# Score maxima taken as scaled, negated minima in the mask instruction, and mean squares moved from VectorE to GpSimd

## The chip, the cores and the metric

The kernel runs on one core of one Trainium2 chip, as one program. The metric is the device time of one execution in microseconds. One execution in the middle of such runs was profiled: its trace gives every instruction of TensorE (PE, with its weight loads as PEld), VectorE (DVE), ScalarE (ACT), GpSimd (POOL) and SyncE (SP, which issues the DMAs) with its start and its duration.

## The reference

The reference is a two-layer decoder trunk on x of shape (1, 256, 1024) in float32. Layer A is causal differential attention with 8 heads, each with two score maps c = 0, 1 of head dimension 64; layer B is dilated sliding-window attention with 16 heads in three groups of keys. Each layer is followed by a squared-ReLU MLP of width 4096. What matters here:

```
rms_norm(y, g) = y * rsqrt(mean(y*y) + EPS) * g        # over each head's 64 columns for q and k
A: s = q k^T * 64^-0.5, masked with -inf above the diagonal;  p = softmax(s)
   a = p[c=0] - lam * p[c=1];  o = rms_norm(a v, sub_gain) * (1 - lam_init)   # over 128 columns
B: s = q k^T * 64^-0.5 for three key groups, masked; m = max(s); p = exp(s - m);
   outputs of the groups mixed by their softmax denominators (one softmax over all groups)
x = x + att @ w_o;   x = x + square(relu(rms_norm(x) @ w_up)) @ w_down
```

## The kernel before

All matrix products are done in split form: each float32 operand is a high part and a low part, and three products are summed (high x high, high x low, low x high). The weights are split while the kernel runs. `Weights.split_half` (L73) lets ScalarE copy the high part of half a weight chunk (`whi`, L82) and VectorE subtract it from the raw chunk (`wlo`, L83); 272 such pairs are spread over the whole kernel, ahead of the products that use them. SyncE fetches the raw chunks by DMA.

The order of the stages is layer A, its output projection, MLP 0, layer B, its output projection, MLP 1. In A the loop runs over 8 heads, in B over 8 pairs of heads. For each, TensorE computes the projections (`gemm`, L297, products on L292 to L294), `qk_rows` (L310) makes normalised and rotated rows of q and k, and a generator, `attn_A` or `attn_B`, is started that does the attention of that head in steps. A generator yields numbers (`WAIT_A`, `WAIT_B`): so many ticks later its next step is put into the program. A tick comes after each half of a projection, so the attention of one head lies between the projection products of the next. The program is then planned by a scheduler that orders the instructions of each engine by their place in the program and by when it reckons that their operands are ready; each engine works through its own queue in that order, and waits at its head.

`qk_rows`, called twice per head in A and four times per pair in B (48 calls), works so: ScalarE squares (L315), VectorE multiplies the rows by the tables into `T` (L317) and sums the squares (`ss`, L321), VectorE forms the mean square plus a term, `ms` (L323), GpSimd adds the rotated halves (L328), raises `ms` to -0.5 (`f`, L332) and multiplies (`qn`, L334). Later TensorE transposes `qn` (L357), and ScalarE and VectorE split the transpose into `th` and `tl` (L340, L341), from which the scores are computed (`scores2`, L350).

The scores are masked by one VectorE instruction (`masked`, L369): it adds the mask to the scores in PSUM, writes the sum and takes its maximum over the row, `mx`. A tiny VectorE instruction then makes `nm`, minus the maximum times 64^-0.5 (L538 in A, L616 in B). ScalarE's exponential takes `nm` as its bias and 64^-0.5 as its scale, and sums the denominators (L541 in A, L618 in B). In B the reciprocal of the denominators (`rd`, L621) and the scaling of the probabilities (L623) follow, and then the transposes L632, the products with v (L646), and, for each pair of heads, a sum `oT` on GpSimd (L651), which ScalarE and VectorE split (L340, L341). In A the two maps are first combined (L545 to L549), transposed (L554) and multiplied by v (L565, L566); the output row is squared with a row sum (L574), its mean square `ms` formed on VectorE (L576), raised to -0.5 on GpSimd (`ors`, L578), applied on ScalarE (L580), and transposed (L584). `cf[:, :, 1]` (L547) is EPS times the square of the first map's denominator, which L576 adds.

The output projection's products are L402 to L404; the MLP's are L435, L437 and L488 to L490.

Of the kernel before, what the change touches and what calls it, by code (L numbers as in the profile page):

```python
# [10 lines left out]
F32 = mybir.dt.float32  # L11
F32R = mybir.dt.float32r
AF = mybir.ActivationFunctionType
ALU = mybir.AluOpType
AX = mybir.AxisListType

P = 128
S = 256
# [3 lines left out]
HD = 64  # L22
# [80 lines left out]
def trunk(ctx, tc, a):  # L103
# [206 lines left out]
    def qk_rows(ps, nsub, eps, tab):  # L310


        n = nsub * HD
        sq = wk.tile([P, 384], F32, name="sq", tag="sq")
        nc.scalar.activation(sq[:, :n], ps[:, :n], AF.Square)  # L315
        T = wk.tile([P, 2, 384], F32, name="T", tag="T")
        nc.vector.tensor_tensor(T[:, :, :n].rearrange("p c (h d) -> p c h d", h=2),  # L317
                                ps[:, None, :n].to_broadcast([P, 2, n]).rearrange("p c (h d) -> p c h d", h=2),
                                tab, op=ALU.mult)
        ss = small.tile([P, 8], F32, name="ss", tag="ss")  # L320
        nc.vector.reduce_sum(ss[:, :nsub], sq[:, :n].rearrange("p (h d) -> p h d", d=HD), axis=AX.X)  # L321
        ms = small.tile([P, 8], F32, name="ms", tag="ms")
        nc.vector.tensor_scalar(ms[:, :nsub], ss[:, :nsub], 1.0 / HD, eps, op0=ALU.mult, op1=ALU.add)  # L323
        u = T[:, 0]
        t1 = T[:, 1, :n]
        swapped = bass.AP(tensor=t1.tensor, offset=t1.offset + HD // 2,
                          ap=[t1.ap[0], [HD, nsub], [-(HD // 2), 2], [1, HD // 2]])
        nc.gpsimd.tensor_tensor(  # L328
            u[:, :n].rearrange("p (h a d) -> p h a d", a=2, d=HD // 2),
            T[:, 0, :n].rearrange("p (h a d) -> p h a d", a=2, d=HD // 2), swapped, op=ALU.add)  # L330
        f = small.tile([P, 8], F32, name="f", tag="f")
        nc.gpsimd.tensor_tensor(f[:, :nsub], ms[:, :nsub], half[:, :nsub], op=ALU.pow)  # L332
        qn = wk.tile([P, 384], F32, name="qn", tag="qn", bufs=6)
        nc.gpsimd.tensor_tensor(  # L334
            qn[:, :n].rearrange("p (h d) -> p h d", d=HD), u[:, :n].rearrange("p (h d) -> p h d", d=HD),
            f[:, :nsub, None].to_broadcast([P, nsub, HD]), op=ALU.mult)
        return qn
# [27 lines left out]

    KALL = slice(S, 2 * S)

    def masked(out, ps, m, init, mx):
        nc.vector.tensor_tensor_reduce(out, ps, m, 1.0, init, ALU.add, ALU.max, mx)  # L369


    def boundary(group, add, outs, ssx, first):
# [149 lines left out]
    def attn_A(hd, qr, kr, vt, oh, ol):  # L522
        yield WAIT_A[0]
        T = qk_T(qr, kr, (0, P))
        yield WAIT_A[1]
        mx = small.tile([P, 4], F32, name="mx", tag="mx")
        den = small.tile([P, 2, 2], F32, name="den", tag="den")
        sm = wk.tile([P, 2, 3 * P], F32, name="smA", tag="sm")
        scs = [wps(), wps()]
        scores2([sc[:, 0:S] for sc in scs], T, block(1), KALL)  # L530
        scores2([sc[:, S:S + P] for sc in scs], T, block(0), slice(S, S + P))
        for c in range(2):
            sc = scs[c]
            masked(sm[:, c, 0:S], sc[:, 0:S], mask[:, 8:10, :].rearrange("p b k -> p (b k)"),
                   -3e38, mx[:, 2 + c:3 + c])
            masked(sm[:, c, S:S + P], sc[:, S:S + P], mask[:, 9, :], -3e38, mx[:, c:c + 1])
        nm = small.tile([P, 4], F32, name="nm", tag="nm")
        nc.vector.tensor_scalar(nm, mx, -(HD ** -0.5), None, op0=ALU.mult)  # L538
        for c in range(2):
            for q, cols in ((1, slice(0, S)), (0, slice(S, S + P))):  # L540
                nc.scalar.activation(sm[:, c, cols], sm[:, c, cols], AF.Exp, bias=nm[:, 2 * q + c:2 * q + c + 1],  # L541
                                     scale=HD ** -0.5, accum_out=den[:, q, c:c + 1])

        cf = small.tile([P, 2, 2], F32, name="cf", tag="cf")
        nc.vector.reciprocal(cf[:, :, 0], den[:, :, 1])  # L545
        nc.vector.scalar_tensor_tensor(cf[:, :, 0], cf[:, :, 0], nlam, den[:, :, 0], op0=ALU.mult, op1=ALU.mult)
        nc.vector.scalar_tensor_tensor(cf[:, :, 1], den[:, :, 0], EPS, den[:, :, 0], op0=ALU.mult, op1=ALU.mult)  # L547
        for q, cols in ((1, slice(0, S)), (0, slice(S, S + P))):
            nc.vector.scalar_tensor_tensor(sm[:, 0, cols], sm[:, 1, cols], cf[:, q, 0:1], sm[:, 0, cols],  # L549
                                           op0=ALU.mult, op1=ALU.add)  # L550
        yield WAIT_A[2]
        pp = wps()
        for i in range(3):
            nc.tensor.transpose(pp[:, block(i)], sm[:, 0, block(i)], ident)  # L554
        p2 = wk.tile([P, 2, 3, P], F32R, name="pA", tag="p2")
        ph, pl = p2[:, 0], p2[:, 1]
        with tc.high_priority(100):
            split(ph, pl, pp[:, :384].rearrange("p (b q) -> p b q", b=3))
        yield WAIT_A[3]
        po = wps()  # L560
        for q in range(2):
            o2 = po[:, q * 2 * P:(q + 1) * 2 * P]
            for j in range(q + 1):
                b = j if q else 2
                nc.tensor.matmul(o2, ph[:, b], vt[:, j], start=j == 0, stop=False)  # L565
                nc.tensor.matmul(o2, pl[:, b], vt[:, j], start=False, stop=j == q)  # L566
        pov = po.rearrange("p (q l d) -> p q l d", q=2, l=2)
        oc = wk.tile([P, 2, P], F32, name="oc", tag="sq")
        nc.scalar.activation(oc, pov[:, :, 1, :], AF.Copy)
        orow = wk.tile([P, 2, P], F32, name="orow", tag="oT")  # L570
        nc.vector.tensor_tensor(orow, pov[:, :, 0, :], oc, op=ALU.add)
        oss = small.tile([P, 2], F32, name="oss", tag="oss")
        for q in range(2):
            nc.scalar.activation(oc[:, q, :], orow[:, q, :], AF.Square, accum_out=oss[:, q:q + 1])  # L574
        ms = small.tile([P, 8], F32, name="ms", tag="ms")
        nc.vector.scalar_tensor_tensor(ms[:, :2], oss, 1.0 / P, cf[:, :, 1], op0=ALU.mult, op1=ALU.add)  # L576
        ors = small.tile([P, 2], F32, name="ors", tag="ors")
        nc.gpsimd.tensor_tensor(ors, ms[:, :2], half[:, :2], op=ALU.pow)  # L578
        for q in range(2):
            nc.scalar.activation(orow[:, q, :], orow[:, q, :], AF.Copy, scale=ors[:, q:q + 1])  # L580
        yield WAIT_A[4]
        pt = wps()
        for q in range(2):
            nc.tensor.transpose(pt[:, block(q)], orow[:, q, :], ident)  # L584

        ptv = pt[:, :S].rearrange("p (m h l) -> p h m l", h=2, l=2)
        for t in range(NT):
            o = oh[:, hd, block(t)].rearrange("p (m l) -> p m l", l=2)
            nc.scalar.activation(o, ptv[:, t], AF.Copy, scale=sgain)
            nc.vector.scalar_tensor_tensor(ol[:, hd, block(t)].rearrange("p (m l) -> p m l", l=2), ptv[:, t], sgain,  # L590
                                           o.bitcast(F32), op0=ALU.mult, op1=ALU.subtract)
# [4 lines left out]
    def attn_B(hp, qr, kr, vts, oh, ol):  # L596
        yield WAIT_B[0]
        T0, T1, T2 = [qk_T(qr, kr, (c, c)) for c in (P, 0, 2 * P)]
        yield WAIT_B[1]
        mxs = [small.tile([P, 2], F32, name="mx", tag="mx") for _ in range(2)]  # L600
        sms = [wk.tile([P, 2, 4 * P], F32, name="sm", tag="sm") for _ in range(2)]
        for b in range(2):
            own = slice(S + b * P, S + (b + 1) * P)
            scs = [wps(), wps()]
            scores2([sc[:, 0:S] for sc in scs], T0, block(b), KALL)
            scores2([sc[:, S:S + P] for sc in scs], T1, block(b), own)
            scores2([sc[:, S + P:] for sc in scs], T2, block(b), own)
            for hh in range(2):
                masked(sms[hh][:, b, :], scs[hh], mask[:, 4 * b:4 * b + 4, :].rearrange("p b k -> p (b k)"),
                       -3e38, mxs[hh][:, b:b + 1])  # L610
            yield WAIT_B[2 + b]
        for hh in range(2):
            sm = sms[hh]
            den = small.tile([P, 2], F32, name="den", tag="den")
            nm = small.tile([P, 2], F32, name="nm", tag="nm")
            nc.vector.tensor_scalar(nm, mxs[hh], -(HD ** -0.5), None, op0=ALU.mult)  # L616
            for b in range(2):
                nc.scalar.activation(sm[:, b, :], sm[:, b, :], AF.Exp, bias=nm[:, b:b + 1], scale=HD ** -0.5,  # L618
                                     accum_out=den[:, b:b + 1])
            rd = small.tile([P, 2], F32, name="rd", tag="rd")  # L620
            nc.vector.reciprocal(rd, den)  # L621
# [209 lines left out]
```

## Time and profile before

| what | value |
|---|---|
| median of 3 runs | 800.8 us (800.39 to 802.36) |
| the profiled execution | 801.55 us, of which the span of instructions 799.5 us |
| TensorE busy | 772.1 us, 97% |
| VectorE busy | 581.1 us, 73%, 985 instructions |
| ScalarE busy | 467.0 us, 58% |
| GpSimd busy | 190.9 us, 24%, 191 instructions |
| mean share of the 16 DMA engines in q1 | 46.0% |

Times in the rows are microseconds from the start of the span, unless marked as ns. Busy time is a union, so that overlapping instructions count once; products on TensorE are pipelined and overlap by more than half. A wait is idle time of an engine ahead of an instruction, with the name of what released it behind "<-". The granted clock of TensorE (PEclk) is a share of full speed. Layer A with its output projection lies at about 10 to 135 us, MLP 0 up to 315, layer B with its projection up to 615, MLP 1 to the end.

### The profile page before, as it was taken

To read this page: it belongs to the slowest core of one execution; us is meant where nothing else is said; L and a number is where in the kernel's file an instruction comes from. 1 tells how busy PE (TensorE), PEld (TensorE's weight loads), DVE (VectorE), ACT (ScalarE), POOL (GpSimd) and SP (SyncE) were. 2 spreads that over 40 slices of the span, in tenths; PEclk is the share of its full clock that TensorE was granted. 3 is DMA by queue.
4 is the path that set the end of the run, shared out by engine and by line. 5 is a ranking of instruction groups with operands and counts; after the bars stand their busy time and mean duration, and the time that the engine had idled before them with its cause. 6 is when DMAs were issued, how large, how long until landed. Compare 5 with 4: busy or idle time off the path is not lost.

```text
span 799.5 us, 11766 instructions
## 1 busy us (share of the span) xinstructions
PE 772.1 (97%) x4408; PEld 686.7 (86%) x4408; DVE 581.1 (73%) x985; ACT 467.0 (58%) x851; POOL 190.9 (24%) x191
## 2 busy tenths in 40 slices
PE   6999989999999999999999999999997999999998
PEld 6898967888888888999999999999886888888886
DVE  3998987666656666998888888888767666556663
ACT  5667777544444445657586674857766544444441
POOL 2553531300000000555336354363611000000000
PEclk9999999999999999999999999999999999999999
DMA  8643445445555542554443434434442455545531
GB/s 300 229 143 123 158 155 164 169 171 197 198 176 207 171 184 90 187 198 154 136 153 113 157 121 157 158 119 172 159 158 106 158 186 182 210 170 199 187 130 52
DMA packets 22328, 131.12 MB, mean 164 GB/s; under 512 B 2560, under 2 KB 3328, under 8 KB 13056
## 3 DMA queue, kind: packets, MB, share of 16 engines
q1 hardware_dynamic: 22272, 130.38, 46.0%
q8 instruction: 34, 0.56, 0.3%
q14 instruction: 22, 0.18, 0.1%
HBM read 129.32 MB, written 1.05 MB: 163 GB/s over the span
## 4 chain that ended last, share of the span: by engine, by line
PE 64%; DVE 17%; ACT 12%; issue 3%; POOL 2%; DMA 1%; SPq 0%; POOLq 0%; DVEq 0%; ACTq 0%
PE wps L435 15%; PE wps L437 7%; PE acc L488 7%; PE acc L489 7%; PE acc L490 7%; DVE wlo L83 5%; PE acc L292 4%; PE acc L294 4%; PE acc L293 4%; ACT whi L82 4%; ACT sm L618 2%; DVE sm L369 2%; PE wps L632 2%; DVE T L317 2%; ACT smA L541 2%
## 5 line engine op out<-in xcount | busy, mean ns | idle before, releaser
L83 DVE TENSOR_TENSOR wlo<-raw,whi 128x1024 fp32r<-128x1024 f32 (+1 forms) x272 | 307.0, 1138 | 153.9 <-ACT whi L82 153.7
L82 ACT ACTIVATE whi<-raw 128x1024 fp32r<-128x1024 f32 (+1 forms) x272 | 258.9, 957 | 211.1 <-issue 74.9
L435 PE MATMUL wps<-hT,whi 128*128 128x512 f32 x512 | 182.2, 399 | 2.0 <-DVE hT L271 2.0
L437 PE MATMUL wps<-hT,wlo 128*128 128x256 f32 x512 | 142.9, 280 | 0.0
L435 PEld LDWEIGHTS wps<-hT,whi 128*128 128x128 f32 x512 | 95.9, 188 | 26.0 <-DVE hT L271 3.2
L328 POOL TENSOR_TENSOR T<-T 128x384 f32<-128x384 f32 (+1 forms) x48 | 44.4, 924 | 280.5 <-DVE ms L243 181.6
L488 PE MATMUL acc<-whi,u 128*128 128x512 f32 x256 | 100.4, 392 | 0.3 <-ACT u L340 0.3
L489 PE MATMUL acc<-wlo,u 128*128 128x512 f32 x256 | 100.0, 391 | 0.0
L490 PE MATMUL acc<-whi,u 128*128 128x512 f32 x256 | 98.9, 389 | 0.0
L437 PEld LDWEIGHTS wps<-hT,wlo 128*128 128x128 f32 x512 | 96.6, 189 | 1.4
L292 PE MATMUL acc<-whi,hT 128*128 128x384 f32 x256 | 88.8, 349 | 0.3 <-ACT whi L82 0.2
L292 PE MATMUL acc<-whi,hK 128*128 128x384 f32 x256 | 87.6, 343 | 0.0
L293 PE MATMUL acc<-wlo,hT 128*128 128x384 f32 x256 | 86.3, 337 | 1.1 <-DVE wlo L83 1.1
L294 PE MATMUL acc<-whi,hT 128*128 128x384 f32 x256 | 86.2, 337 | 0.0
L294 PE MATMUL acc<-whi,hK 128*128 128x384 f32 x256 | 85.8, 335 | 0.0
L293 PE MATMUL acc<-wlo,hK 128*128 128x384 f32 x256 | 85.7, 335 | 0.0
L332 POOL TENSOR_TENSOR f<-ms,half 128x6 f32<-128x6 f32 (+1 forms) x48 | 68.2, 1422 | 4.6 <-DVE ms L323 3.1
L488 PEld LDWEIGHTS acc<-whi,u 128*128 128x128 f32 x256 | 48.1, 188 | 11.7 <-ACT u L340 1.2
L490 PEld LDWEIGHTS acc<-whi,u 128*128 128x128 f32 x256 | 48.1, 188 | 10.6 <-DVE u L341 0.4
L489 PEld LDWEIGHTS acc<-wlo,u 128*128 128x128 f32 x256 | 48.1, 188 | 8.8
L293 PEld LDWEIGHTS acc<-wlo,hT 128*128 128x128 f32 x256 | 48.6, 190 | 1.4 <-DVE wlo L83 1.4
L292 PEld LDWEIGHTS acc<-whi,hT 128*128 128x128 f32 x256 | 48.6, 190 | 1.4 <-ACT whi L82 0.5
(117 smaller groups left out, 1204.9 us busy)
## 6 DMA issues: line engine op xcount, KB each, us to landing
raw<-in_wB SPq DMA_DIRECT2D x48, 768.0 KB, 4.2
raw<-in_wup SPq DMA_DIRECT2D x32, 1024.0 KB, 4.8
raw<-in_wdn SPq DMA_DIRECT2D x32, 1024.0 KB, 4.8
raw<-in_wA SPq DMA_DIRECT2D x15, 768.0 KB, 4.3
raw<-in_woA SPq DMA_DIRECT2D x4, 1024.0 KB, 4.8
raw<-in_woB SPq DMA_DIRECT2D x4, 1024.0 KB, 4.8
early<-in_x SPq DMA_DIRECT2D x2, 512.0 KB, 5.3
x<-in_xp SPq DMA_DIRECT2D x1, 1024.0 KB, 7.5
```

What stands on the lines that cost most here:

```text
L82: self.nc.scalar.activation(hi[:, :n], raw, AF.Copy)
L83: self.nc.vector.tensor_tensor(lo[:, :n], raw, hi[:, :n].bitcast(F32), op=ALU.subtract)
L292: nc.tensor.matmul(ps, h[:, kt, 0, tok], wh[:, c], start=kt == 0, stop=False)
L293: nc.tensor.matmul(ps, h[:, kt, 0, tok], wl[:, c], start=False, stop=False)
L294: nc.tensor.matmul(ps, h[:, kt, 1, tok], wh[:, c], start=False, stop=kt == KT - 1)
L328: nc.gpsimd.tensor_tensor(u[:, :n].rearrange("p (h a d) -> p h a d", a=2, d=HD // 2), T[:, 0, :n].rearrange("p (h a d) -> p h a d", a=2, d ...
L332: nc.gpsimd.tensor_tensor(f[:, :nsub], ms[:, :nsub], half[:, :nsub], op=ALU.pow)
L435: nc.tensor.matmul(o, wh[:, c], self.h[:, kt].rearrange("p l s -> p (l s)"), start=kt == 0, stop=False, skip_group_check=True)
L437: nc.tensor.matmul(o[:, 0:S], wl[:, c], self.h[:, kt, 0, :], start=False, stop=kt == KT - 1, skip_group_check=True)
L488: nc.tensor.matmul(ps, uh[:, tok], dh[:, c], start=first, stop=False)
L489: nc.tensor.matmul(ps, uh[:, tok], dl[:, c], start=False, stop=False)
L490: nc.tensor.matmul(ps, ul[:, tok], dh[:, c], start=False, stop=last)
```

## The change

The mask instruction now multiplies the masked sum by -(64^-0.5), writes that, and takes the minimum, which is at once `nm`; the separate `nm` instructions (8 in A, 16 in B) are gone and the exponential has scale -1. The mean square `ms` in `qk_rows` is computed by GpSimd. In A the term with the denominator is squared on ScalarE (scale EPS^0.5), the factor 1/128 of the output row's mean square moves into the scale of the ScalarE square, and the sum of both is taken on GpSimd.

```diff
@@ qk_rows
-        nc.vector.tensor_scalar(ms[:, :nsub], ss[:, :nsub], 1.0 / HD, eps, op0=ALU.mult, op1=ALU.add)
+        nc.gpsimd.tensor_scalar(ms[:, :nsub], ss[:, :nsub], 1.0 / HD, eps, op0=ALU.mult, op1=ALU.add)
@@ masked
-    def masked(out, ps, m, init, mx):
-        nc.vector.tensor_tensor_reduce(out, ps, m, 1.0, init, ALU.add, ALU.max, mx)
+    def masked(out, ps, m, nm):
+        nc.vector.tensor_tensor_reduce(out, ps, m, -(HD ** -0.5), 3e38, ALU.add, ALU.min, nm)
@@ attn_A
-        nm = small.tile([P, 4], F32, name="nm", tag="nm")
-        nc.vector.tensor_scalar(nm, mx, -(HD ** -0.5), None, op0=ALU.mult)
...
-                                     scale=HD ** -0.5, accum_out=den[:, q, c:c + 1])
+                                     scale=-1.0, accum_out=den[:, q, c:c + 1])
...
-        nc.vector.scalar_tensor_tensor(cf[:, :, 1], den[:, :, 0], EPS, den[:, :, 0], op0=ALU.mult, op1=ALU.mult)
+        nc.scalar.activation(cf[:, :, 1], den[:, :, 0], AF.Square, scale=EPS ** 0.5)
...
-            nc.scalar.activation(oc[:, q, :], orow[:, q, :], AF.Square, accum_out=oss[:, q:q + 1])
+            nc.scalar.activation(oc[:, q, :], orow[:, q, :], AF.Square, scale=P ** -0.5,
+                                 accum_out=oss[:, q:q + 1])
...
-        nc.vector.scalar_tensor_tensor(ms[:, :2], oss, 1.0 / P, cf[:, :, 1], op0=ALU.mult, op1=ALU.add)
+        nc.gpsimd.tensor_tensor(ms[:, :2], oss, cf[:, :, 1], op=ALU.add)
@@ attn_B
-            nm = small.tile([P, 2], F32, name="nm", tag="nm")
-            nc.vector.tensor_scalar(nm, mxs[hh], -(HD ** -0.5), None, op0=ALU.mult)
...
-                nc.scalar.activation(sm[:, b, :], sm[:, b, :], AF.Exp, bias=nm[:, b:b + 1], scale=HD ** -0.5,
+                nc.scalar.activation(sm[:, b, :], sm[:, b, :], AF.Exp, bias=nms[hh][:, b:b + 1], scale=-1.0,
```

## Rows read from the trace of the kernel before

**Rows 1.** The page's first part: busy time and share of each engine.
```profile
PE 772.1 (97%) x4408; PEld 686.7 (86%) x4408; DVE 581.1 (73%) x985; ACT 467.0 (58%) x851; POOL 190.9 (24%) x191
```
**Rows 2.** The list of waits: who waited for whom, total us, times, longest.
```profile
ACT smA L541 <- DVE nm L538: 14.6, 7, 2.8
...
PE wps L350 <- DVE tl L341: 4.1, 4, 1.9
...
PE wps L632 <- ACT sm L623: 3.9, 6, 1.0
...
PE acc L402 <- ACT oTh L340: 2.6, 1, 2.6
...
PE wps L357 <- POOL qn L334: 0.6, 1, 0.6
```
**Rows 3.** VectorE's timeline in one head of A: start, duration, instruction, [idle before].
```profile
83.42 0.41 DVE L369 CUSTOM_DVE_ANT_0 smA<-wps,mask 128x256 f32<-128x256 f32 x1
...
84.52 1.31 DVE L83 TENSOR_TENSOR wlo<-raw,whi 128x768 fp32r<-128x768 f32 x1
85.76 0.16 DVE L538 TENSOR_SCALAR nm<-mx 128x4 f32<-128x4 f32 x1
...
87.85 0.17 DVE L545 RECIPROCAL cf<-den 128x2 f32<-128x2 f32 x1 [0.72 <-ACT smA L541]
...
90.57 0.68 DVE L341 TENSOR_TENSOR tl<-wps,th 128x512 fp32r<-128x512 f32 x1
```
**Rows 4.** ScalarE's timeline in the same head.
```profile
85.95 0.51 ACT L541 ACTIVATE smA<-smA,nm 128x256 f32<-128x256 f32 x1 [2.68 <-DVE nm L538]
```
**Rows 5.** TensorE's timeline in the same head.
```profile
85.26 0.60 PE L357 MATMUL wps<-ident,qn 128*128 128x128 f32 x4
...
91.31 0.39 PE L350 MATMUL wps<-th,tl 64*128 64x256 f32 x2 [0.94 <-DVE tl L341]
```
**Rows 6.** GpSimd's timeline in the same head.
```profile
83.32 1.01 POOL L332 TENSOR_TENSOR f<-ms,half 128x4 f32<-128x4 f32 x1
84.41 0.61 POOL L334 TENSOR_TENSOR qn<-T,f 128x256 f32<-128x256 f32 x1
```
**Rows 7.** Timelines of four engines in one pair of heads of B.
```profile
392.16 0.73 POOL L651 TENSOR_TENSOR oT<-ot 64x256 f32<-64x256 f32 x1
...
398.76 0.28 DVE L616 TENSOR_SCALAR nm<-mx 128x2 f32<-128x2 f32 x2
...
398.96 0.72 ACT L618 ACTIVATE sm<-sm,nm 128x512 f32<-128x512 f32 x1 [1.83 <-DVE nm L616]
...
403.19 0.21 DVE L621 RECIPROCAL rd<-den 128x2 f32<-128x2 f32 x2
...
403.64 2.55 ACT L623 ACTIVATE sm<-sm,rd 128x512 f32<-128x512 f32 x4
...
404.40 1.27 PE L632 MATMUL wps<-ident,sm 128*128 128x128 f32 x8 [0.56 <-ACT sm L623]
```
**Rows 8.** Windows: stretch, length, busy of each engine, PEclk, DMA share, GB/s.
```profile
60.00:100.00 40.00, 37.16 (x250) 35.79 (x249) 36.68 (x105) 29.25 (x89) 17.71 (x23) 1.00 0.40 141
100.00:140.00 40.00, 35.85 (x184) 27.41 (x183) 32.38 (x82) 30.22 (x86) 8.41 (x11) 0.96 0.46 160
...
106.00:107.00 1.00, 1.00 (x2) 0.81 (x3) 1.00 (x5) 0.00 (x0) 0.90 (x2) 0.50 0.96 401
```
**Rows 9.** ScalarE's timeline in the last pair of heads of B.
```profile
594.89 0.72 ACT L618 ACTIVATE sm<-sm,nm 128x512 f32<-128x512 f32 x1 [2.94 <-DVE nm L616]
```
**Rows 10.** Instruction groups: busy us, mean ns of one, idle before and its releaser.
```profile
L323 DVE TENSOR_SCALAR ms<-ss,rB 128x6 f32<-128x6 f32 x32 | 9.9, 309 | 0.2
...
L576 DVE SCALAR_TENSOR_TENSOR ms<-oss,cf 128x2 f32<-128x2 f32 x8 | 1.2, 151 | 0.6 <-ACT oc L574 0.6
...
L203 ACT ACTIVATE le<-ls 128x2 f32<-128x2 f32 x1 | 0.2, 189 | 0.0
...
L172 POOL MEMSET half<- 128x8 f32 x1 | 0.1, 104 | 0.3 <-POOLq L821 0.3
```

More of the change, by code (lines that the diff above doesn't have):

```diff
@@ L525, in attn_A @@
         yield WAIT_A[1]
-        mx = small.tile([P, 4], F32, name="mx", tag="mx")
+        nm = small.tile([P, 4], F32, name="nm", tag="nm")
         den = small.tile([P, 2, 2], F32, name="den", tag="den")
@@ L534, in attn_A @@
             masked(sm[:, c, 0:S], sc[:, 0:S], mask[:, 8:10, :].rearrange("p b k -> p (b k)"),
-                   -3e38, mx[:, 2 + c:3 + c])
-            masked(sm[:, c, S:S + P], sc[:, S:S + P], mask[:, 9, :], -3e38, mx[:, c:c + 1])
-        nm = small.tile([P, 4], F32, name="nm", tag="nm")
-        nc.vector.tensor_scalar(nm, mx, -(HD ** -0.5), None, op0=ALU.mult)
+                   nm[:, 2 + c:3 + c])
+            masked(sm[:, c, S:S + P], sc[:, S:S + P], mask[:, 9, :], nm[:, c:c + 1])
         for c in range(2):
@@ L599, in attn_B @@
         yield WAIT_B[1]
-        mxs = [small.tile([P, 2], F32, name="mx", tag="mx") for _ in range(2)]
+        nms = [small.tile([P, 2], F32, name="nm", tag="nm") for _ in range(2)]
         sms = [wk.tile([P, 2, 4 * P], F32, name="sm", tag="sm") for _ in range(2)]
@@ L609, in attn_B @@
                 masked(sms[hh][:, b, :], scs[hh], mask[:, 4 * b:4 * b + 4, :].rearrange("p b k -> p (b k)"),
-                       -3e38, mxs[hh][:, b:b + 1])
+                       nms[hh][:, b:b + 1])
             yield WAIT_B[2 + b]
```

## The prediction, written before the changed kernel was run

> **What bounds the kernel now.** I read the page's busy shares first [rows 1]: TensorE is busy 97% of the span, so a change elsewhere can pay only where TensorE waits, or where its clock is low. The second view was the list of waits [rows 2]. The reader is to see in it that TensorE's waits have few names. The score matmuls of layer A (L350) wait 4.1 us in all, four times, for VectorE's `tl`, the low half of the split transposes. The probability transposes of layer B (L632) wait 3.9 us, six times, for ScalarE's normalised scores. Behind the last head of B the output projection (L402) waits 2.6 us. The two stages of the MLP do not stand in this list. The same view says who is late for whom one step earlier: ScalarE's exponentials of A wait 14.6 us, in seven heads, for VectorE's `nm`, the instruction that the change removes.
>
> Third, timelines of one head of A, engine by engine. VectorE has finished the first of four masked maxima (L369) at 83.83 us and the last when it takes up a `wlo` subtraction at 84.52; only behind that comes the scaling `nm`, at 85.76 [rows 3]. ScalarE sits idle 2.68 us and starts the first exponential at 85.95 [rows 4]. VectorE in turn idles 0.72 us for the exponentials before the reciprocal at 87.85, and reaches `tl` at 90.57 [rows 3]. TensorE asked for `tl` 0.94 us before it could begin L350 [rows 5]. So the loop that paces A is VectorE's queue, lengthened by a wait for ScalarE, which waited for VectorE. TensorE is next behind it, 0.94 us per head earlier. In B the loop has more room, and only the end of it shows: `nm` ends about 398.96, the exponentials start then after 1.83 us of idle time, the reciprocals come at 403.19, the normalisation at 403.64, and TensorE has waited 0.56 us at 404.40 [rows 7].
>
> Fourth, the clock. From 106 to 107 us the granted clock is 0.50, the lower level (1.2 GHz), while over 100 to 140 us it is 0.96 on average, and 1.00 over the 40 us before [rows 8], so 40 x 0.04 = 1.6 us of full-speed work is lost there. What TensorE did before the fall is the longest of the L350 waits, 1.9 us [rows 2].
>
> **The change part by part.** All sums are against the profiled execution, 801.55 us (span 799.5, 2.05 around it); it lies 0.75 us above the median of the runs.
>
> *nm goes; the masked instruction delivers it.* The mask instruction keeps its form and its read of the accumulator, with another constant and minimum for maximum, so I cost that at nothing (one constant against another; no row shows a difference either way, and I see no reason for one). What goes is 8 instructions of 0.16 us and 16 of 0.14 (two took 0.28) [rows 3, 7], 3.5 us of VectorE, but what counts is the release. In A the exponentials no longer wait for the `wlo` ahead of `nm`. ScalarE was free at 85.95 - 2.68 = 83.27, the first maximum is there at 83.83, so the first exponential starts 2.1 us earlier, and the four, which took 87.85 - 85.95 = 1.9 us, end near 85.8, with the new ScalarE square of the denominator among them near 86.0. The reciprocal then finds them done when VectorE gets to it. VectorE's queue to `tl` shortens by the 0.72 us wait, `nm` 0.16, and the two small products, each priced by the one shown, 0.15 [rows 3, 10]: 1.18 us. TensorE's wait was 0.94. So it goes, and TensorE itself is late next, by 0.24 us, more when two mean squares leave VectorE too. I expect the 4.1 us of L350 to go whole.
>
> *The clock.* If the wait of 1.9 us before it goes or shrinks below a microsecond, I expect no fall there: 1.6 us. Bounds: nothing, or all 1.6. I take all, since the falls that I see follow a gap of about two microseconds, and the shorter waits of the same heads, 0.94 us, are followed by none [rows 8].
>
> *Layer B.* The first of the four exponentials needs only the first block's maximum, and ScalarE is free 1.83 us before; so it runs in that idle time. But the normalisation needs the reciprocals, and these stand in VectorE's queue at 403.19 behind other work. That queue loses the `nm` pair, 0.28, and two mean squares of 0.31 each [rows 10]: 0.9 us if they count in full, 0.5 if they overlap their neighbours. TensorE's wait is 0.56, longest 1.0 [rows 2, 7]. Something may be given back: GpSimd now takes a mean square ahead of the sum `oT` at 392.16 [rows 7], for which ScalarE and then VectorE wait in their queues. Bounds of the gain: 0.9 and 3.9 us. I take three quarters, 2.9.
>
> *Mean squares on GpSimd.* 48 in the row helper and 8 in A. VectorE loses 48 of about 0.3 us and 8 of 0.15 [rows 10]. GpSimd's own price is not in this trace. Below, a memset of eight columns took 0.104 us [rows 10]; above, the power on 128x4, one of the slowest things that it does per element, took 1.01 us [rows 6]. A multiply-add is nearer to the memset in work, but must read; I take 0.30 us. In A this lies near the path: `qn` ends at 84.41 + 0.61 = 85.02 and TensorE's transposes of it begin at 85.26 [rows 5, 6], 0.24 us of slack. After the change VectorE's products, which start GpSimd's chain, come 1.2 us earlier, TensorE comes 0.94 us earlier, and two mean squares of c each stand ahead of the last `qn`. The slack is 0.24 + 1.2 - 0.94 - 2c = 0.5 - 2c. With c = 0.30 TensorE waits 0.1 us in each of some six heads: 0.6 us back, and 0.3 more at the one head where it waited 0.6 for `qn` already [rows 2]. In B the code transposes `qn` a whole projection later, so only `oT` counts, as above.
>
> The Trainium skill speaks against this move: "GPSIMD Engine Reference", section "Performance versus the Vector engine", holds that two-input elementwise work takes GpSimd about twice as long as VectorE. By that an estimate for c would be about 0.6 us and the slack above would turn into a wait of 0.7 us per head. No row here shows a mean square on GpSimd, so the trace neither agrees nor disagrees yet; the rival below carries it.
>
> *The denominator's square on ScalarE, and the sum on GpSimd (A only).* Eight ScalarE instructions near 0.19 us, the row of the 128x2 exponential [rows 10]; hidden in ScalarE's idle time, 2.68 us per head [rows 4]; without that cover they would delay the exponentials by 0.19 each, 1.5 us in all. The GpSimd sum replaces a VectorE instruction between the same two neighbours; what it costs is a step of 0.1 to 0.3 us for one of 0.15, taken as nothing.
>
> *End of B.* The last head's exponentials are in the open: ScalarE idles 2.94 us for `nm` until 594.89 [rows 9]. One exponential of 0.72 us moves into that idle time and the next starts when its own maximum is there, half a microsecond or so earlier: 1.2 us (bounds 0 and 2.6, the wait of L402 [rows 2]).
>
> Sum: 4.1 + 1.6 + 2.9 + 1.2 - 0.9 = 8.9 us; 801.55 - 8.9 = 792.6, said as 792.5.
>
> **The rivals.**
> *VectorE's queue hides most of it.* Exponentials earlier, but `tl` and the reciprocals still sit behind weight subtractions. Then A gains only the removed instructions (0.46 of 0.94, so half of 4.1), the clock still falls, and B gains 1.5: with 0.6 at the end 4.1 us, 797.4. For it: in rows 3 a `wlo` stood in front of `nm`, and such work is moved freely. Against it: the 0.72 us that VectorE waited are measured, not argued. Chance 0.18.
> *GpSimd paces A.* c = 0.56, half way between the bounds. Each of six heads waits 2 x 0.56 - 0.5 = 0.62 us, 3.7 in all, which eats the 4.1; I let the clock's fall stay; B loses 0.26 of its gain per head more, leaving 1.4, and 0.6 at the end: 2.4 us, 799.1. That is the case of the rule named above. For it: the slack of 0.24 us. Chance 0.15, together with others that end in no change.
> *Slower: a mean square costs GpSimd what a power costs,* c = 1.01. In A the wait would be 1.5 us a head against 0.94 before, six times 0.58 = 3.5 us worse; in B `oT` comes a microsecond late, more than the 0.56 that was gained, 0.4 a head, 2.6 us; 6.1 us in all, 807.6. It decides from c = 0.72, where 2c - 0.5 reaches 0.94. For it: the power's time per column shows how slow this engine can be. Against it: the power itself is what is dear there; the plain products on 64 times as many columns took 0.61 us [rows 6]. Chance 0.10.
>
> **How the numbers follow.** About 0.3% (2.4 us) is what a measurement of this kernel can tell from no change. Forecast, 788.5 to 796: 0.57; the first rival, near 797.4: 0.18, both faster by more than that; no change 0.15; slower 0.10. So faster 0.75, same 0.15, slower 0.10. The lower end has all bounds at their best: 4.1 + 1.6 + 3.9 + 2.6 = 12.2 us, 789.4, less the 0.75 by which a median run is shorter, 788.6. The upper end leaves out the slower rival and part of no change: 799.3.
>
> **What would show it.** In the profile after: no wait of ScalarE for `nm`, exponentials beginning within 0.1 us of a mask instruction; the L350 waits under 1 us in sum; no granted clock of 0.50 between 100 and 115 us; L632's waits under 1.5 us in sum; the reciprocals of A without a wait of 0.7 us. A mean square on GpSimd over 0.5 us, or waits of L357 for `qn` above 2 us in sum, would put the second rival in its place; L350's wait for `tl` left at half would be the first. What would make the forecast wrong altogether is a VectorE or ScalarE queue whose order has changed so that another instruction stands where `nm` stood.

## The result, and the profile after

The changed kernel took 841.72 us (median of 4 runs, 841.47 to 842.47) against 801.36 us of the kernel before on the same chip: a ratio of 1.0505 [1.0487, 1.0523], 40 us slower. The prediction was 792.5 us with a range up to 799.3: the sign was wrong.

The page's first part after, to be read against [rows 1]:

```profile
span 839.4 us, 11737 instructions
...
PE 780.0 (93%) x4408; PEld 690.9 (82%) x4408; DVE 578.1 (69%) x897; ACT 468.7 (56%) x859; POOL 222.2 (26%) x247
```

The span grew by 39.9 us. TensorE runs the same 4408 products. Its time outside them grew from 799.5 - 772.1 = 27.4 us to 839.4 - 780.0 = 59.4, by 32.0 us; its busy time grew by 7.9 us. By stage, from the starts of the first products of each MLP: layer A takes 7.7 us longer (137.1 to 144.8 us), MLP 0 with layer B 30.6 (479.6 us before, 510.2 after), MLP 1 1.6.

The list of waits after, which answers to [rows 2] (L644 is the old L646, which waits for `p`, the transposed probabilities in split form; L630 is the old L632, L616 the old L618, L649 the old L651, and L370, the mask instruction, now makes `nm`):

```profile
ACT oTh L340 <- POOL oT L649: 41.3, 8, 6.2
DVE oTl L341 <- ACT oTh L340: 31.9, 8, 4.9
ACT sm L616 <- DVE nm L370: 29.9, 16, 2.3
...
PE wps L644 <- DVE p L341: 16.6, 8, 3.5
...
PE wps L630 <- ACT sm L621: 12.5, 12, 1.3
ACT smA L540 <- DVE nm L370: 12.3, 7, 2.4
PE wps L357 <- POOL qn L334: 11.6, 7, 3.8
```

Three of its lines before that [rows 2] does not show:

```profile
ACT oTh L340 <- POOL oT L651: 24.7, 8, 3.5
...
DVE oTl L341 <- ACT oTh L340: 14.5, 8, 2.0
...
PE wps L646 <- DVE p L341: 0.9, 1, 0.9
```

Three names make up TensorE's new idle time: 16.6 + 12.5 + 11.6 = 40.7 us, where the kernel before had 0.9 + 3.9 + 0.6 = 5.4 of them. The wait of L350 fell from 4.1 to 0.8. So the small term of the forecast is there, and three others outweigh it. One step earlier, the first two lines show ScalarE and VectorE idle at the heads of their queues for the sum `oT`, 41.3 and 31.9 us, where before it was 24.7 and 14.5. The third shows that the exponentials still wait for `nm`, which the forecast said they would not: 29.9 us in B, and 12.3 in A, where it was 14.6.

**One pair of heads of B after.** A block is 128 of the 256 query rows, so a pair of heads has four masks and four exponentials: block 0 of both heads, then block 1 of both. ScalarE, VectorE and TensorE (start, duration, instruction, [idle before]), to be read against [rows 7]:

```profile
442.93 0.42 ACT L340 ACTIVATE oTh<-oT 128x256 fp32r<-128x256 f32 x1 [6.23 <-POOL oT L649]
445.31 0.73 ACT L616 ACTIVATE sm<-sm,nm 128x512 f32<-128x512 f32 x1 [1.97 <-DVE nm L370]
...
446.04 0.71 ACT L616 ACTIVATE sm<-sm,nm 128x512 f32<-128x512 f32 x1
...
446.74 1.57 ACT L82 ACTIVATE whi<-raw 128x768 fp32r<-128x768 f32 x2
450.08 0.72 ACT L616 ACTIVATE sm<-sm,nm 128x512 f32<-128x512 f32 x1 [1.77 <-DVE nm L370]
```

```profile
443.38 0.43 DVE L341 TENSOR_TENSOR oTl<-oT,oTh 128x256 fp32r<-128x256 f32 x1 [4.87 <-ACT oTh L340]
...
445.19 0.69 DVE L370 CUSTOM_DVE_ANT_0 sm<-wps,mask 128x512 f32<-128x512 f32 x1
...
447.60 1.83 DVE L83 TENSOR_TENSOR wlo<-raw,whi 128x768 fp32r<-128x768 f32 x2 [1.72 <-ACT whi L82]
449.35 0.68 DVE L370 CUSTOM_DVE_ANT_0 sm<-wps,mask 128x512 f32<-128x512 f32 x1
```

```profile
452.07 0.66 PE L630 MATMUL wps<-ident,sm 128*128 128x128 f32 x4 [0.98 <-ACT sm L621]
...
460.77 1.22 PE L644 MATMUL wps<-p,v 128*128 128x512 f32 x6 [2.13 <-DVE p L341]
```

ScalarE and VectorE in the pair of [rows 7] before, where the masks are L369:

```profile
393.25 1.78 ACT L82 ACTIVATE whi<-raw 128x768 fp32r<-128x768 f32 x2
...
394.58 0.68 DVE L369 CUSTOM_DVE_ANT_0 sm<-wps,mask 128x512 f32<-128x512 f32 x1
...
397.55 0.68 DVE L369 CUSTOM_DVE_ANT_0 sm<-wps,mask 128x512 f32<-128x512 f32 x1
```

The reader is to see a ring of two engines. ScalarE takes the exponentials of block 0 as soon as their minimum is there (445.31), as the forecast wanted. But it takes both heads' ahead of two high halves `whi` (446.74). VectorE's next instructions are the two low halves `wlo` of these weights, and it sits 1.72 us idle for them (447.60). The masks of block 1 stand behind the `wlo` in its queue and begin at 449.35, 4.77 us after those of block 0 (444.58). In the kernel before the same distance was 2.97 us (394.58 to 397.55), since ScalarE had made the `whi` (393.25) in the time in which it had nothing else to do. Then ScalarE waits 1.77 us for a minimum again (450.08), and TensorE 0.98 us for the scaled scores and 2.13 us for `p`. An engine works through its queue in order, so an instruction taken up early delays everything behind it, on the other engine too.

**Layer A after.** GpSimd and VectorE in one head, against [rows 3, 6], and TensorE, against [rows 5]:

```profile
84.58 0.73 POOL L328 TENSOR_TENSOR T<-T 128x256 f32<-128x256 f32 x1
85.42 0.27 POOL L323 TENSOR_SCALAR ms<-ss,rA 128x4 f32<-128x4 f32 x1
...
88.99 0.85 POOL L323 TENSOR_SCALAR ms<-ss,rA 128x4 f32<-128x4 f32 x1
...
91.02 0.61 POOL L334 TENSOR_TENSOR qn<-T,f 128x256 f32<-128x256 f32 x1
```

```profile
84.42 0.41 DVE L321 TENSOR_REDUCE ss<-sq 128x4 f32<-128x256 f32 x1
85.59 0.69 DVE L317 TENSOR_TENSOR T<-acc,tabA 128x512 f32<-128x512 f32 x1 [0.76 <-ACT sq L315]
...
88.68 1.02 DVE L83 TENSOR_TENSOR wlo<-raw,whi 128x768 fp32r<-128x768 f32 x1
```

```profile
91.69 0.55 PE L357 MATMUL wps<-ident,qn 128*128 128x128 f32 x3 [1.61 <-POOL qn L334]
```

GpSimd's first line of the head of [rows 6], before:

```profile
79.95 1.60 POOL L328 TENSOR_TENSOR T<-T 128x256 f32<-128x256 f32 x2
```

A mean square takes GpSimd 0.27 us while VectorE is idle (84.83 to 85.59), and 0.85 us while VectorE subtracts weights (88.68 to 89.70). GpSimd's two rows of a head take from 84.58 to 91.63, 7.05 us; before it was 79.95 to 85.02, 5.07. TensorE waits 1.61 us for the second `qn`. In the whole trace the 48 mean squares fall into two groups: 31 that no weight subtraction overlaps take 0.27 to 0.28 us, with other VectorE instructions beside them too, and 17 that one overlaps take 0.85 to 2.18 us. The means lie between (mean ns), against [rows 10]:

```profile
L323 POOL TENSOR_SCALAR ms<-ss,rB 128x6 f32<-128x6 f32 x32 | 20.1, 629 | 3.2
...
L323 POOL TENSOR_SCALAR ms<-ss,rA 128x4 f32<-128x4 f32 x16 | 10.0, 627 | 1.6
```

**The clock.** Windows after (stretch, length, busy of PE, PEld, DVE, ACT, POOL, granted clock, DMA share, GB/s), against [rows 8]:

```profile
20.00:60.00 40.00, 35.66 (x217) 34.06 (x216) 32.13 (x70) 24.09 (x61) 22.15 (x29) 0.91 0.52 186
...
100.00:140.00 40.00, 33.39 (x185) 26.97 (x185) 29.89 (x75) 28.70 (x85) 15.69 (x21) 1.00 0.37 131
...
23.00:24.00 1.00, 0.00 (x0) 0.00 (x0) 1.00 (x3) 0.70 (x1) 0.96 (x1) 0.50 0.60 92
...
580.00:620.00 40.00, 34.20 (x216) 31.36 (x214) 28.85 (x42) 23.85 (x41) 18.80 (x18) 0.96 0.37 132
620.00:660.00 40.00, 34.91 (x189) 28.01 (x187) 24.25 (x43) 24.38 (x47) 2.19 (x3) 0.91 0.31 106
```

The fall to 0.50 (1.2 GHz) at 106 us is gone, as forecast. Another stands at 23 us, in the 3.8 us wait for the first `qn` of A, and costs more: 40 x 0.09 = 3.6 us against 1.6. The kernel before has a second fall, at the end of B, which [rows 8] does not show:

```profile
580.00:620.00 40.00, 35.98 (x204) 29.12 (x203) 27.89 (x49) 26.18 (x48) 4.60 (x4) 0.96 0.38 132
```

It comes behind the 2.6 us wait of L402 and costs 40 x 0.04 = 1.6 us. After, there are two such falls: one behind a 3.5 us wait for `p` (580 to 620 us, 1.6), and one at the same wait as before (620 to 660 us, 40 x 0.09 = 3.6). In sum 8.8 us against 3.2, so the clock makes 5.6 of the 7.9 us by which TensorE's busy time grew.

### The profile page after: what moved, and what is told of

Its sections match the earlier page's. It is cut to its first block, busy times and chain, and to the rows that moved or that the text cites. A ratio compares the mean times of both kernels' runs of the same rounds, so it can differ in the third digit from the quotient of the medians.

```text
span 839.4 us, 11737 instructions
## 1 busy us (share of the span) xinstructions
PE 780.0 (93%) x4408; PEld 690.9 (82%) x4408; DVE 578.1 (69%) x897; ACT 468.7 (56%) x859; POOL 222.2 (26%) x247
## 4 chain that ended last, share of the span: by engine, by line
PE 60%; DVE 13%; ACT 13%; POOL 8%; issue 4%; DMA 1%; SPq 0%; POOLq 0%; DVEq 0%; ACTq 0%
PE wps L436 14%; PE acc L489 7%; PE acc L490 7%; PE wps L438 7%; PE acc L491 7%; DVE wlo L83 6%; ACT whi L82 5%; PE acc L294 4%; PE acc L292 4%; PE acc L293 4%; POOL f L332 2%; ACT sm L616 2%; POOL T L328 2%; ACT sm L621 2%; POOL qn L334 2%
## 5 line engine op out<-in xcount | busy, mean ns | idle before, releaser
L83 DVE TENSOR_TENSOR wlo<-raw,whi 128x1024 fp32r<-128x1024 f32 (+1 forms) x272 | 314.0, 1165 | 171.6 <-ACT whi L82 170.7
L328 POOL TENSOR_TENSOR T<-T 128x384 f32<-128x384 f32 (+1 forms) x48 | 54.0, 1126 | 306.1 <-DVE ms L243 181.9
L332 POOL TENSOR_TENSOR f<-ms,half 128x6 f32<-128x6 f32 (+1 forms) x48 | 59.8, 1247 | 4.0
```

What stands on the lines that cost most here:

```text
L83: self.nc.vector.tensor_tensor(lo[:, :n], raw, hi[:, :n].bitcast(F32), op=ALU.subtract)
L328: nc.gpsimd.tensor_tensor(u[:, :n].rearrange("p (h a d) -> p h a d", a=2, d=HD // 2), T[:, 0, :n].rearrange("p (h a d) -> p h a d", a=2, d ...
```

## The experiments

Two theories. **GpSimd**: the fold of the scale into the mask gains what was forecast, and the mean squares on GpSimd cost more than that. **Queue orders**: no instruction costs much; the planner, which orders every queue by when it reckons operands ready, laid the queues out otherwise, and the time goes into waits at the heads of queues. The planner is the scheduler that orders the queues; the fold is the change of the mask and of the exponentials; the tail of A is what changes behind A's exponentials. An edge, below, fixes the order of two instructions in one engine's queue. Every ratio is against the kernel before, run again on the same chip.

**The parts alone, planned afresh.** The fold alone (masks, exponentials; mean squares and tail of A as before):

```diff
+        nc.vector.tensor_tensor_reduce(out, ps, m, -(HD ** -0.5), 3e38, ALU.add, ALU.min, nm)
...
-            nc.vector.tensor_scalar(nm, mxs[hh], -(HD ** -0.5), None, op0=ALU.mult)
```

> The kernel before with the fold alone: the mask instruction delivers nm, mean squares stay on VectorE, the tail of A as before. If GpSimd's mean squares (their time or the queue order that they bring) are the whole loss: 790 to 797 us, the exponentials no longer 2 us late, L350's waits in A and L632's in B mostly gone. If the fold itself brings the loss, by other queue orders on ScalarE and VectorE: 815 us or more.

826.05 us, 1.0305 [1.029, 1.032]. Its own waits:

```profile
ACT sm L615 <- DVE nm L370: 30.4, 16, 3.0
...
PE wps L643 <- DVE p L341: 17.6, 8, 4.5
```

An edit that takes VectorE instructions away, and nothing from GpSimd or to it, costs 25 us. The ring described above stands in this trace just so: two exponentials (434.80, 435.52) ahead of the `whi` (436.23), and 4.76 us from the masks of block 0 (434.08) to those of block 1 (438.84). GpSimd is not the cause of it: ScalarE waits for `oT` as long as before, 24.7 us. Of the 25.3 us by which the span grew (799.5 to 824.8), 10.7 are TensorE's busy time (772.1 to 782.8): behind some of the waits its clock falls, to 0.97 on average from 400 to 500 us, where it was 1.00.

The mean squares of the row helper alone:

```diff
-        nc.vector.tensor_scalar(ms[:, :nsub], ss[:, :nsub], 1.0 / HD, eps, op0=ALU.mult, op1=ALU.add)
+        nc.gpsimd.tensor_scalar(ms[:, :nsub], ss[:, :nsub], 1.0 / HD, eps, op0=ALU.mult, op1=ALU.add)
```

> The kernel before with the 48 mean squares of the row helper on GpSimd and nothing else. If they are the whole loss: 840 to 850 us, GpSimd's queue with oT behind both rows as in the changed kernel. If the fold is the loss: 795 to 810 us.

827.02 us, 1.0327 [1.0308, 1.0345], between the two bands that were expected. TensorE's L632 waits 16.7 us in sum, up to 3.8. GpSimd now finishes one row before it begins the next, and `oT` comes behind both rows: ScalarE waits 41.3 us for it, as in the changed kernel.

The tail of A alone (square on ScalarE, sum on GpSimd):

```diff
...
-        nc.vector.scalar_tensor_tensor(ms[:, :2], oss, 1.0 / P, cf[:, :, 1], op0=ALU.mult, op1=ALU.add)
+        nc.gpsimd.tensor_tensor(ms[:, :2], oss, cf[:, :, 1], op=ALU.add)
```

> The kernel before with only layer A's tail changed: denominator squared on ScalarE, sum on GpSimd. Either theory: 798 to 805 us, within 0.5% of before. Above 810 us only if GpSimd's sum in front of its power holds up A by itself.

807.1 us, 1.0077 [1.006, 1.0094], 2.1 us above the band of either theory. L357 waits 4.1 us for `qn`, in four heads, and L402 waits 2.8 us for VectorE at the end of A, where it was 0.2. The order of the queues has changed here too.

The whole change with the row helper's mean squares back on VectorE:

```diff
-        nc.gpsimd.tensor_scalar(ms[:, :nsub], ss[:, :nsub], 1.0 / HD, eps, op0=ALU.mult, op1=ALU.add)
+        nc.vector.tensor_scalar(ms[:, :nsub], ss[:, :nsub], 1.0 / HD, eps, op0=ALU.mult, op1=ALU.add)
```

> The changed kernel with the mean squares of the row helper back on VectorE: fold and tail of A stay. If GpSimd's mean squares are the whole loss: 788 to 797 us. If the loss needs only the fold or the tail: 820 us or more.

824.76 us, 1.0292 [1.0266, 1.0319]: the fold's loss again. Three parts lose by themselves, so each either costs by itself or reorders by itself. Their losses (24.4, 25.4 and 5.5 us) come to more than the 40 us of the whole, so they overlap.

**The order alone.** The kernel before, no instruction changed; two edges that carry an order and no semaphore make GpSimd's queue the one of the mean squares alone: a row's sum behind the last row's `qn`, and `oT` behind both.

```diff
+        with (tc.issue_after(last_qn[-1]) if last_qn else ExitStack()):
+            nc.gpsimd.tensor_tensor(u..., T..., swapped, op=ALU.add)
...
+            with tc.issue_after(last_qn[-1]):
+                nc.gpsimd.tensor_tensor(oT[rows, :], ot[rows, 0], ot[rows, 1], op=ALU.add)
```

> The kernel before, no instruction changed; edges only make GpSimd serve the rows one by one (the next row's add behind the last row's multiply) and oT behind both, as the moved mean squares do. Order theory: 812 to 828 us, with L632 waiting about 2 us per pair of heads. If GpSimd's time is what counts: 799 to 805 us.

827.99 us, 1.0335 [1.0314, 1.0356], within the interval of the mean squares alone, with the same instructions as the 801 us kernel. In this trace GpSimd's instructions come in the order of the changed kernel, one by one, but for the mean squares; TensorE's and ScalarE's come in that of the kernel before, and on VectorE six weight subtractions have changed places with a neighbour. Its list of waits:

```profile
ACT oTh L343 <- POOL oT L655: 45.3, 8, 6.9
...
DVE oTl L344 <- ACT oTh L343: 28.9, 8, 4.4
...
PE wps L635 <- ACT sm L626: 19.2, 6, 3.5
```

`oT` late on GpSimd leaves ScalarE and VectorE idle at the heads of their queues, the masks behind them are late, and TensorE waits for the scaled scores. The changed kernel has 41.3 us of such idle time.

**The parts, in the queues of the kernel before.** Now the planner's freedom is taken away: every instruction of an engine is tied, again by order alone, to the one ahead of it in the kernel before. A new instruction stands directly ahead of the one that uses it (a mean square ahead of its power) or behind its producer. In the traces of the five runs that are held so (three here, two further down) the orders of TensorE, VectorE, ScalarE and GpSimd are those of the kernel before, but for the instructions that went and came. In outline:

```diff
+    for engine, perm in queues_of_before:
+        for p, q in zip(perm, perm[1:]):
+            tc.add_manual_dep(mine[q], mine[p].name, NoSync)
```

The fold alone:

> The fold alone, with every engine's queue tied, by edges that order and do not wait, to exactly the order that the kernel before has, nm left out. If the planner's new queue orders are the whole loss of the fold (826 us): 793 to 800 us, L632's wait in B gone and nothing new behind it. If the folded instruction or the earlier exponentials cost by themselves: 815 us or more.

795.65 us, 0.9929 [0.9916, 0.9943]: 6 us faster than before, and 30 us faster than the same instructions as planned.

The row helper's mean squares alone:

> The 48 mean squares on GpSimd, each directly ahead of its power, all queues else in the order of the kernel before. This keeps GpSimd's added time and takes away the new order. Order theory: 798 to 804 us. If GpSimd's time is the loss of the move (827 us): 820 us or more; between the two, the time's share is read off, near 0.4 us per row on oT and qn.

800.66 us, 0.9993 [0.9984, 1.0002], no different from before. No L350 wait is left in the list, and L357's wait for `qn` has grown to 6.3 us.

The whole change:

> All of the change, with the queues of the kernel before: mean squares directly ahead of their powers, the sum ahead of its power, the denominator's square behind the four exponentials. Order theory: 790 to 798 us, which is what the prediction reckoned with. If the instructions themselves cost: 830 us or more.

801.11 us, 0.9999 [0.9987, 1.001], 3 us above the band of the order theory. All of the 40 us is gone with the order alone. But the fold's gain is gone too, and this trace shows where (its L388, L354 and L363 are L357, L323 and L332):

```profile
PE wps L388 <- POOL qn L365: 7.5, 6, 2.8
```

```profile
81.76 1.06 POOL L354 TENSOR_SCALAR ms<-ss,rA 128x4 f32<-128x4 f32 x1
82.90 1.02 POOL L363 TENSOR_TENSOR f<-ms,half 128x4 f32<-128x4 f32 x1
...
84.71 0.85 POOL L354 TENSOR_SCALAR ms<-ss,rA 128x4 f32<-128x4 f32 x1
85.65 1.69 POOL L363 TENSOR_TENSOR f<-ms,half 128x4 f32<-128x4 f32 x1
```

VectorE subtracts weights from 81.74 to 82.69 and from 84.44 to 86.47. A mean square beside it takes 0.85 to 1.06 us, not 0.27, and the power 1.69, not 1.02. In B no wait of a pair of heads is left in this trace but 0.6 us for `p` at the end of B. So the remaining cost should lie in A. The next pair tests that.

**A version that gains.** The fold, and GpSimd's mean squares in B only, tail of A as before, queues of before:

```diff
+        ms_engine = nc.gpsimd if nsub == 6 else nc.vector
+        ms_engine.tensor_scalar(ms[:, :nsub], ss[:, :nsub], 1.0 / HD, eps, op0=ALU.mult, op1=ALU.add)
```

> The fold, and the mean squares on GpSimd in part B only (a row's tile of 384 columns); in part A they stay on VectorE, and the tail of A stays as before. Every queue in the order of the kernel before. Theory (the two parts gain once the queues stand still, and GpSimd's mean squares cost only in A, where each head waits for qn): A as in the fold with the queues of before (795.65), B without a TensorE wait per pair, as in the whole change with the queues of before: 793.5 to 795.5. Rival (a mean square on GpSimd costs wherever it stands, a term of B that the waits of the whole change hid): 796 to 800. In the trace: waits of TensorE for qn at L358 in A as before (0.3 in sum), none over 0.3 us for sm or p in a pair of B.

792.29 us, 0.9882 [0.9867, 0.9897], 1.2 us under the band of the theory and 3.7 under its rival's. Of the 3.4 us between this and the fold alone, the lists of waits show 0.4, the last wait of L632; where the rest lies stays open. The same with the changed tail of A:

> The same, and the tail of A's heads as in the change (the eps square on ScalarE, the mean square of the output row on GpSimd, 8 heads). Theory: the tail is off TensorE's path when the queues stand still, within 1.5 us of the run above, 793.5 to 796.5. Rival (the tail lengthens the chain from the output row to the next head's rows on GpSimd, some 0.3 us a head and 2 to 4 in sum, as the tail alone with a free planner cost 6 us): 796 to 800.

791.89 us, 0.9878 [0.9865, 0.9892], under its band as well, the fastest of all and no different from the one above. A line of its page (its span is 790.1 us), and its list of waits:

```profile
PE 770.7 (98%) x4408; PEld 686.4 (87%) x4408; DVE 569.7 (72%) x913; ACT 467.6 (59%) x859; POOL 209.4 (27%) x231
```

```profile
PE acc L435 <- ACT oTh L372: 2.6, 1, 2.6
...
PE wps L676 <- DVE p L373: 0.6, 1, 0.6
PE wps L389 <- POOL qn L366: 0.4, 1, 0.4
```

L350 and L632 have left the list, and `qn` costs 0.4 us instead of 7.5. The engine of A's 16 mean squares is the one difference between this kernel and the whole change in the same queues, so they cost the 9 us between 801.11 and 791.89: 7.1 us by the waits for `qn`, and the clock, which in the whole change falls at the end of A (0.96 over 100 to 140 us) behind a 2.8 us wait for `qn`.

**One edge against the ring.** The fold alone, the planner free but for the exponentials of B, which are queued behind the high half of the last weights:

```diff
+                with tc.issue_after(W.last_hi):
                     nc.scalar.activation(sm[:, b, :], sm[:, b, :], AF.Exp, bias=nms[hh][:, b:b + 1], scale=-1.0,
```

> The fold alone with the planner free, but for one order: the exponentials of B are queued on ScalarE behind the high half of the last weights that were loaded ahead of them. Theory (the fold loses because ready exponentials are queued ahead of the weights' high halves, and these hold VectorE's low halves, the masks of block 1 and then the normalised scores back): most of the 25 us comes back, 797 to 805, and the wait of TensorE for p at L644 shrinks from 2.1 us a pair to under 0.8. Rival (it is the sum of many small reorderings, and no single order mends it): 815 to 827, with the wait in its place.

803.76 us, 1.0022 [1.001, 1.0034], inside the band of the order theory. ScalarE now makes the `whi` ahead of the exponentials, and TensorE's wait for `p` fell from 17.6 to 1.5 us:

```profile
394.58 1.74 ACT L82 ACTIVATE whi<-raw 128x768 fp32r<-128x768 f32 x2
```

With this one edge 22 of the fold's 25 us come back. The planner has laid other places out anew as well: just ahead of a pair's first `p` ScalarE makes one `whi`, as before, where the fold alone has two (in seven of the eight pairs). So what the edge does by itself is not told apart from what the planner made of it; GpSimd's order is that of the fold alone. What it still lacks against the fold in the queues of before, 8 us, lies in other orders: its list has 3.3 us for `qn` and 1.2 for L350 in A, where that trace has 0.5 and none.

Left open: which of the planner's reckonings makes it turn these orders over; its inner working was not examined. Nor was the kernel before run with the fold's order, since its `nm` needs the maxima of both blocks and so cannot be queued that way.

## Why the prediction was wrong, point by point

- *The step that failed* is in the part on layer B: "The first of the four exponentials needs only the first block's maximum, and ScalarE is free 1.83 us before; so it runs in that idle time", and, in the part on the mean squares, "so only `oT` counts". Both reckon with the queues of before. The first exponentials did start with their minimum, but two heads' worth of them displaced the `whi`, on which VectorE's queue, and in it the next masks, depended; and GpSimd's rows were laid one behind the other, which put `oT` and with it two whole queues back (the order alone: 1.0335). The gain of 2.9 us became a loss of 30.6, with TensorE waiting 16.6 us for `p` and 12.5 for the scaled scores. With the old order held the same change takes 801.11 us instead of 841.72. That a queue's order could change stood in the last paragraph as what would overturn the forecast, but no rival carried it: a change of dependencies goes through the planner, so it deserved a mechanism, a price and a chance of its own.
- *The exponentials' release in A, 4.1 us*: right with the queues held; L350 is in the list of none of the traces with the queues of before. In the changed kernel 0.8 is left, but TensorE waits earlier, for `qn`.
- *The clock, 1.6 us*: right where no new wait came in. Over 100 to 140 us the granted clock is 1.00 after and in the best version, whose busy time of TensorE is 772.1 - 770.7 = 1.4 us less; in the version without the changed tail, at 1.00 there too, it is only 0.1 less. In the whole change with the queues held it is 0.96 there again, behind a new wait for `qn`. In the changed kernel new long waits brought new falls, 5.6 us of the 7.9 by which busy time grew, and the fall at the end of B, which the kernel before had too, was not reckoned with.
- *B, 2.9 us*: with the queues held, L632's 3.9 us fell to 0.4 by the fold alone, and to nothing with the mean squares: the upper bound, 3.9.
- *The mean squares, 0.9 us back in A*: mis-sized. c = 0.30 holds only where VectorE leaves GpSimd alone (0.27); beside weight subtractions c is 0.85 to 1.06 in the head shown, and the power stretches too. With the queues held L357 waits 7.5 us instead of 0.6: 6.9 us back. The trace before could have warned: the power on 128x6 (L332) takes 1.33 us at 389 us and 2.05 at 402. The Trainium skill, "GPSIMD Engine Reference", section "Key points", says that GpSimd shares its SBUF interfaces with VectorE and contends with VectorE instructions that have two SBUF inputs; the trace agrees: `wlo` reads two (`raw`, `whi`), and only the mean squares beside a `wlo` took more than 0.28 us. The rule of that page that the prediction weighed, half of VectorE's speed, stands there for two-input work, and a mean square reads one tensor: alone it took 0.27 us, against a median of 0.22 on VectorE before (0.31 on the mean [rows 10]).
- *The tail of A at nothing*: right with the queues held (791.89 against 792.29); planned afresh it cost 0.8%.
- *The end of B, 1.2 us*: wrong. L402's wait for `oTh` is 2.6 us in every trace; with the queues held only the wait for `p` before it shrank, from 0.9 to 0.6.
- *The rivals*: "GpSimd paces A" had the right place and the right direction, and its 799.1 is close to the 801.11 of the whole change in unchanged queues, in part by luck: it let B's gain shrink, which came in full, and priced A's waits for `qn` at 3.7 us, which were 7.5. The slower rival named a mean square as dear as a power: beside VectorE it nearly is (1.06), but it is not what made the kernel slower.

The sum of 8.9 us, with the 0.9 that was to be given back put at nothing, is 9.8; the version that leaves A's mean squares on VectorE, in unchanged queues, gained 801.8 - 791.89 = 9.9. That they agree so well is in part luck: B gave 3.9 for 2.9 and the end of B 0.3 for 1.2. The mechanism of the fold and of B was right for a program whose order stands still; A's mean squares were mis-sized even there. Two smaller points: the list of waits does hold the MLP (L435, 2.0 us, for `hT`; 1.6 after), and the upper end of the range, 799.3, has no working.

## What to carry to other kernels

When a scheduler lays out the queues, the removal of a tiny instruction changes when later ones are reckoned ready, and so their order on every engine; price a change by its order first, and read it in the timelines as what stands ahead of the instruction that moved. An instruction that may start earlier should not get ahead of one on which another engine's queue depends; tie it there, or hold the old order, before judging the idea itself. And price small work moved to GpSimd by what VectorE does at the same moment.

## What the runs showed of the hardware

- A mean square of 128x4 on GpSimd took 0.27 us with no weight subtraction of VectorE beside it, and 0.85 to 1.64 beside one, which reads two SBUF tiles (changed kernel, 16 of them); a power went from 1.02 to 1.69 us.
- TensorE's clock fell to 0.50 (1.2 GHz) during a wait of 3.8 us in the changed kernel. Not every wait brings a fall: behind B's 2.1 us waits for `p`, one in each pair of heads, the granted clock stayed at 1.00 on average over 400 to 600 us, while in the fold alone, with waits of the same length, it was 0.97 over 400 to 500 us, and in the reordered kernel before, with waits of 3.1 us, 0.95 over 400 to 600. No run here tells what decides.
